# Attention queries in a hybrid encoder: when their tiles are taken

## The chip, the cores and the metric

The kernel runs on one core of a Trainium2 chip. The metric is the device time of one execution in microseconds; the median of several runs is given with its range. A profile of one execution shows when each instruction ran on each engine: TensorE (PE, with its weight loads PEld), VectorE (DVE), ScalarE (ACT), GpSimd (POOL) and SyncE (SP), whose queue issues the DMAs.

## The reference, cut to what matters

One step of a two-layer encoder for a prompt of 2048 positions and a sample of 8 x 16 later positions, with the same weights. The first layer computes two mixers from one projection; the change lies in the queries of the first, and the work around it belongs to the second:

```python
z = rms_norm(h, norm_g) @ w_in
a_q, a_k, a_v, a_g, b_qkv, b_g, b_beta, b_alpha = split_cols(z, AB_WIDTHS)
q = rms_norm(a_q.reshape(Bn, T, A_HEADS, A_HEAD_DIM), q_norm)
k = rms_norm(a_k.reshape(Bn, T, A_KV_HEADS, A_HEAD_DIM), k_norm)
o_a = swa_prompt(q, k, v, sinks)            # sample: swa_sample
...
bq = l2_norm(...); bk = l2_norm(...)
o_b, s_new = gated_delta_rule(bq, bk, bv, beta, g, s0, chunk)
o_b = rms_norm(o_b, o_norm) * silu(b_g)
y = h + concatenate([o_a, o_b]) @ w_out
```

The delta rule solves a unit lower triangular system for each chunk. The second layer takes trailing means over 2 to 16 positions, maps them by groups, and adds them behind a gate.

## The kernel before

The positions are worked on in four groups of 128-row blocks (`GROUPS`). Group 0 holds four prompt blocks (0 to 3) and, as block 4, the sample's 128 rows (`samp`, `npb` = 4 prompt blocks, `nb` = 5); groups 1 to 3 hold four prompt blocks each. Each product is three matmuls, of high and low parts (`XH`, `XL`, and `w` split in two), so that a projection of eight slices of the contraction is 24 matmuls. Weights come two ahead by `weight()`: SyncE loads `wst`, ScalarE makes the high part (L471), VectorE and GpSimd the low part (L475).

A group runs keys, then for each of two pairs of heads the second mixer's keys (`b_keys`), its queries (`b_queries`) and the attention's queries (`a_queries`); for pair 0 `a_queries` stands ahead of `b_queries`, for pair 1 behind it. Then come gate projections (L702 to L704), the output projection and the pooling layer.

`a_queries(jp)` runs over the blocks that `tok_major` yields. For each block there are 24 matmuls, L1305 to L1307, into one of two PSUM banks `pj`. ScalarE copies the bank into the tile `z` (L1400; L1397 for the sample's block) and squares it (L1319). VectorE sums the squares (L1320, L1324 or L1322), GpSimd takes the power -1/2 (L501, tile `rsa`) and scales `z` twice (L1328, L1329). Later `qcols` transposes `z` on TensorE by four matmuls into one of two banks `tp` (L1412), and ScalarE (L1414) and VectorE (L1416) write the high and low part into `qs`. The sample's block goes through L1407 and L1408 into `A`.

Beside it the second mixer runs as jobs. `b_chain` inverts the triangular blocks: VectorE makes 31 steps of two instructions (L1019, L1020) on the tile `Xb`, copies it transposed into `XbT` (L1024), SyncE writes both to DRAM (L1026, L1027) and reads them back in another layout (L1035, L1037), and small matmuls (L1046 to L1081) and copies finish the inverse. Then `b_recur` walks the chunks (L1172 to L1220), and in group 0 also the sample's, one head after the other: L1172, L1241, L1249, L1190, L1255 and L1261 on TensorE, and on VectorE L1182, L1192, L1196, L1198, L1259 and eight L1264, with L1272, then L501 (tile `ro`) and L1277 on GpSimd to end a head. When `a_queries(1)` of group 0 runs, the sample's recurrence of pair 0 and the inverse of pair 1 are under way.

What sets the order: the code emits instructions by hand. `tick` moves a virtual clock on with each projection matmul, and jobs and deferred functions (`defer(DEF, qcols)`) run when they are due. Large SBUF tiles come from `slot`, which has 11 big and 6 small ones in two free lists, first in, first out; `drop` puts one back at the end. Where none is free, `slot` calls `progress`, which runs the next deferred function or job ahead of its due time until one is. A tile that was used before is waited for: its new writer waits for the last readers, DMAs among them. Afterwards each engine's instructions are put in an order of their own by the scheduler of the framework.

Of the kernel before, what the change touches and what calls it, by code (L numbers as in the profile page):

```python
# [8 lines left out]
F32R = mybir.dt.float32r  # L9
# [6 lines left out]
P = 128  # L16
# [221 lines left out]
def hybrid_kernel(  # L238
# [50 lines left out]
    def slot(shape, dt=F32):  # L289
        size = 1  # L290
        for s in shape[1:]:
            size *= s
        while True:
            if size <= SMALL and free_small:
                tag = free_small.pop(0)
                break
            if free_big:
                tag = free_big.pop(0)
                break
            if not progress():  # L300
                raise RuntimeError("no slot: " + ", ".join(v[2] for v in held.values()))
        v = sl.tile(list(shape), dt, tag=tag, name=nm(tag), bufs=1)
        held[id(v)] = (tag, v, str(shape))
        return v
# [5 lines left out]
    def drop(*vs):  # L310
        for v in vs:
            tag = held.pop(id(v))[0]
            (free_big if tag[0] == "B" else free_small).append(tag)
# [366 lines left out]
    def group(gix, norm_job):  # L680
        p0, npb, samp = GROUPS[gix]
# [700 lines left out]

        def a_queries(jp):

            qs = [slot([P, 2, 4, P], F32R) for _ in range(2)]
            zs = [slot([P, 2, 4, 2, 64]) for _ in range(2)]
            A = qh = None
            if samp:

                A = slot([P, 2, n])  # L1390
                qh = A[:, :, srow].rearrange("p c (j q) -> p c j q", q=64)
                zs.append(A[:, 0, 0:256].rearrange("p (j g d) -> p j g d", j=2, d=64))
            st["qh", jp] = (qs, qh, A)
            for b, pp in tok_major():
                z = zs[b // 2][:, b % 2] if b < npb else zs[2]
                if b >= npb:
                    S.copy(z.rearrange("p j g d -> p g j d"), pp.rearrange("p (g j d) -> p g j d", g=2, d=64))  # L1397
                    head_norm(z.rearrange("p j g d -> p (j g) d"), 4)
                else:
                    S.copy(z[:, :, 0, :], pp.rearrange("p (i d) -> p i d", d=64))  # L1400
                    head_norm(z[:, :, 0, :], 4, z[:, :, 1, :], qms[:, 4 * jp:4 * jp + 4])

                def qcols(z=z, b=b):
                    pt = psum("tp")
                    if b >= npb:
                        for j in range(2):
                            T_.transpose(pt[:, P * j:P * j + P], z[:, j].rearrange("p g d -> p (g d)"), ident)  # L1407
                        S.mul(qh.rearrange("p c j q -> p j c q"),  # L1408
                              pt[:, 0:256].rearrange("p (j c q) -> p j c q", j=2, q=64), gq8)
                        return  # L1410
                    for i in range(4):
                        T_.transpose(pt[:, P * i:P * i + P], z[:, i].rearrange("p e d -> p (e d)"), ident)  # L1412
                    q = qs[b // 2][:, b % 2].rearrange("p i t -> p (i t)")
                    S.mul(q, pt, gq8)  # L1414
                    low = q[64:128]
                    V.scalar_tensor_tensor(low, pt[64:128], gq8[64:128], f32(low), op0=ALU.mult,  # L1416
                                           op1=ALU.subtract)

                defer(DEF, qcols)

            def end():
                drop(*zs[0:2])
                st["A", jp] = start(a_attend(jp), 0.6)

            defer(DEF + 0.1, end)
# [450 lines left out]
```

## Time and profile before

| what | value |
|---|---|
| median of 3 runs (range) | 1901.49 us (1900.74 to 1903.12) |
| the profiled execution, its own time | 1898.98 us |
| its span | 1897.2 us |
| mean granted clock of TensorE | 0.992 |

The profile's page gives for each engine the busy time, its share of the span and the count of instructions. The slices cut the span in 40 equal parts, each digit the busy share in tenths. The waits group the idle times of an engine by the instruction behind them and by the one that ended them (total us, times, longest). A timeline row is the start, the duration, the engine, the line, the operation with its tiles (out<-in), and in brackets the idle time ahead of it with what ended it. A window row is its length, then the busy time of TensorE, its weight loads, VectorE, ScalarE and GpSimd, each with a count, then TensorE's clock, the DMA share and GB/s.

### The profile page before, as it was taken

Reading aid. Unit: us, or ns where it says so; the run is one execution under the profiler, and the core shown is the slowest. Engines: PE = TensorE matmul, PEld = TensorE weight load, DVE = VectorE, ACT = ScalarE, POOL = GpSimd, SP = SyncE. Lnnn points to the kernel's source line nnn. Section 1 sums busy time; section 2 is a strip of 40 time slices with the busy share of each in tenths; the row PEclk is TensorE's granted clock in tenths of the full one; section 3 lists DMA queues with packets and bytes.
Section 4 is the critical chain, followed back from the end, with each engine's and each line's share of the span. In section 5 each row is a group of like instructions: output and inputs, shape, how many; then the busy total and the mean of one; then the engine's idle time right before and its main releaser. Section 6 shows DMA issues by size and latency. Waiting matters only on the chain.

```text
span 1897.2 us, 30999 instructions
## 1 busy us (share of the span) xinstructions
PE 1824.5 (96%) x11434; PEld 1598.7 (84%) x11434; DVE 1196.4 (63%) x3184; ACT 733.8 (39%) x1883; POOL 498.8 (26%) x628
## 2 busy tenths in 40 slices
PE   6999989999999999999999999999999999999999
PEld 6888888889998888888888988888888988788887
DVE  6797967545664697764445597774345597764342
ACT  4465436323332474262222374261222474261210
POOL 5632451323332522310112413220012413220100
PEclk9998999999999999999999999999999999999999
DMA  7433362756668533435457533435467533435554
GB/s 277 144 133 125 120 226 76 250 195 208 229 234 293 214 119 105 167 118 189 171 204 282 208 115 108 166 130 188 161 217 278 204 117 118 148 134 189 182 189 186
DMA packets 94579, 337.52 MB, mean 178 GB/s; under 512 B 35884, under 2 KB 44332, under 8 KB 64988
## 3 DMA queue, kind: packets, MB, share of 16 engines
q1 hardware_dynamic: 94428, 335.54, 50.8%
q8 instruction: 90, 1.47, 0.3%
q14 instruction: 61, 0.50, 0.1%
HBM read 256.93 MB, written 78.58 MB: 177 GB/s over the span
## 4 chain that ended last, share of the span: by engine, by line
PE 74%; DVE 16%; POOL 3%; issue 3%; ACT 2%; DMA 2%; SPq 0%; DVEq 0%; POOLq 0%; ACTq 0%
PE pj L702 12%; PE pj L704 12%; PE pj L703 12%; PE pj L737 3%; PE pj L735 3%; PE pj L736 3%; PE rc L737 2%; PE rc L735 2%; PE rc L736 2%; DVE tm L1019 2%; DVE A L1020 2%; PE pj L1305 2%; PE pj L1306 2%; PE pj L1307 2%; PE tp L557 1%
## 5 line engine op out<-in xcount | busy, mean ns | idle before, releaser
L702 PE MATMUL pj<-XH,w 128*128 128x512 f32 (+3 forms) x1512 | 546.9, 362 | 5.5 <-ACT cb L876 3.4
L704 PE MATMUL pj<-XH,w 128*128 128x512 f32 (+3 forms) x1512 | 536.2, 355 | 0.0
L703 PE MATMUL pj<-XL,w 128*128 128x512 f32 (+3 forms) x1512 | 535.1, 354 | 0.0
L702 PEld LDWEIGHTS pj<-XH,w 128*128 128x128 f32 x1512 | 288.2, 191 | 33.7 <-ACT cb L876 3.7
L704 PEld LDWEIGHTS pj<-XH,w 128*128 128x128 f32 x1512 | 287.5, 190 | 29.3 <-issue 0.2
L703 PEld LDWEIGHTS pj<-XL,w 128*128 128x128 f32 x1512 | 288.0, 190 | 26.5 <-issue 0.2
L475 POOL TENSOR_TENSOR w<-wst,w 128x640 fp32r<-128x640 f32 (+2 forms) x60 | 105.2, 1754 | 179.0 <-ACT w L471 154.5
L1305 PE MATMUL pj<-w,XH 128*128 128x256 f32 (+1 forms) x368 | 106.8, 291 | 0.3 <-DVE VL L1351 0.3
L1307 PE MATMUL pj<-w,XL 128*128 128x256 f32 (+1 forms) x368 | 104.4, 284 | 0.0
L1306 PE MATMUL pj<-w,XH 128*128 128x256 f32 (+1 forms) x368 | 104.3, 283 | 0.0
L742 DVE TENSOR_TENSOR A<-pj,A 128x512 f32<-128x512 f32 x37 | 25.5, 689 | 101.4 <-PE pj L737 101.4
L737 PE MATMUL pj<-w,B 128*128 128x512 f32 x224 | 87.5, 391 | 0.0
L737 PE MATMUL rc<-w,B 128*128 128x512 f32 x212 | 82.6, 390 | 0.0
L471 ACT CAST w<-wst 128x1024 fp32r<-128x1024 f32 (+1 forms) x60 | 61.2, 1021 | 53.5 <-PE sc L737 42.0
L1723 DVE TENSOR_TENSOR B<-cb 128x526 f32<-128x526 f32 x32 | 24.1, 752 | 75.8 <-ACT cb L1775 75.7
L475 DVE TENSOR_TENSOR w<-wst,w 128x384 fp32r<-128x384 f32 (+2 forms) x60 | 48.1, 804 | 37.3 <-ACT w L471 37.1
L715 DVE SCALAR_TENSOR_TENSOR A<-A,pj 128x512 f32<-128x512 f32 (+1 forms) x33 | 21.1, 639 | 80.1 <-ACT A L714 79.8
L1305 PEld LDWEIGHTS pj<-w,XH 128*128 128x128 f32 x368 | 70.0, 190 | 1.7 <-DVE VL L1351 0.5
L1306 PEld LDWEIGHTS pj<-w,XH 128*128 128x128 f32 x368 | 70.1, 190 | 1.1 <-issue 0.5
L1307 PEld LDWEIGHTS pj<-w,XL 128*128 128x128 f32 x368 | 70.0, 190 | 0.0
L1019 DVE TENSOR_TENSOR tm<-A,A 40x31 f32<-40x31 f32 (+31 forms) x155 | 62.9, 406 | 6.8 <-DMA A<-Ld 4.4
L896 DVE SCALAR_TENSOR_TENSOR B<-cb,taps,B 128x512 f32<-128x512 f32 x78 | 57.8, 741 | 11.9 <-ACT B L885 11.2
(505 smaller groups left out, 4299.0 us busy)
## 6 DMA issues: line engine op xcount, KB each, us to landing
w<-wk SPq DMA_DIRECT2D x168, 1024.0 KB, 4.9
wk<-w SPq DMA_DIRECT2D x56, 1024.0 KB, 6.4
wst<-in_wts SPq DMA_DIRECT2D x56, 512.0 KB, 4.3
A<-in_x SPq DMA_DIRECT2D x22, 512.0 KB, 4.5
w<-wk SPq DMA_DIRECT2D x6, 1056.0 KB, 5.3
B<-in_x SPq DMA_DIRECT2D x12, 512.0 KB, 4.2
w<-wk SPq DMA_DIRECT2D x12, 512.0 KB, 3.3
out_y<-B SPq DMA_DIRECT2D x9, 512.0 KB, 2.6
```

The costliest lines, as they stand in the source:

```text
L471: S.copy(hi, st)
L475: eng.tensor_tensor(lo[:, a:b], st[:, a:b], f32(hi[:, a:b]), op=ALU.subtract)
L702: mm(pp[:, 0:w], wh[:, k, :], xh[:, k, t0:t1], start=(k == 0), stop=False)
L703: mm(pp[:, 0:w], wh[:, k, :], xl[:, k, t0:t1], start=False, stop=False)
L704: mm(pp[:, 0:w], wl[:, k, :], xh[:, k, t0:t1], start=False, stop=(k == KT - 1))
L735: mm(pp, oh[:, tk], wt[0][:, k, :], start=(kk == k == 0), stop=False)
L736: mm(pp, oh[:, tk], wt[1][:, k, :], start=False, stop=False)
L737: mm(pp, ol[:, tk], wt[0][:, k, :], start=False, stop=(kk == k == 1))
L1019: V.tensor_tensor(t3, bc(Lb[:, j + 1:32, j], w), bcm(Xb[:, j, 0:w], r), op=ALU.mult)
L1305: mm(pp[:, 0:N], xh[:, k, tk], wh[:, k % 4, :], start=(k == 0), stop=False)
L1306: mm(pp[:, 0:N], xh[:, k, tk], wl[:, k % 4, :], start=False, stop=False)
L1307: mm(pp[:, 0:N], xl[:, k, tk], wh[:, k % 4, :], start=False, stop=(k == KT - 1))
```

## The change

The tiles of the queries are no longer taken all at the start of `a_queries`. A pair `qs`, `zs` is taken when an even prompt block comes out of its matmuls, `A` when the sample's block does; and a `zs` is dropped by `qcols` of the odd block that uses it last, no longer by `end` after all of them. The lines behind move: L1397 becomes L1398, L1400 L1401, L1407 L1408, L1412 L1413, L1414 L1415, L1416 L1417.

```diff
--- before.py
+++ after.py
@@ -1382,17 +1382,18 @@
 
         def a_queries(jp):
 
-            qs = [slot([P, 2, 4, P], F32R) for _ in range(2)]
-            zs = [slot([P, 2, 4, 2, 64]) for _ in range(2)]
+            qs, zs = [], []
             A = qh = None
-            if samp:
-
-                A = slot([P, 2, n])
-                qh = A[:, :, srow].rearrange("p c (j q) -> p c j q", q=64)
-                zs.append(A[:, 0, 0:256].rearrange("p (j g d) -> p j g d", j=2, d=64))
-            st["qh", jp] = (qs, qh, A)
             for b, pp in tok_major():
-                z = zs[b // 2][:, b % 2] if b < npb else zs[2]
+                if b == npb:
+
+                    A = slot([P, 2, n])
+                    qh = A[:, :, srow].rearrange("p c (j q) -> p c j q", q=64)
+                    zq = A[:, 0, 0:256].rearrange("p (j g d) -> p j g d", j=2, d=64)
+                if b < npb and b % 2 == 0:
+                    qs.append(slot([P, 2, 4, P], F32R))
+                    zs.append(slot([P, 2, 4, 2, 64]))
+                z = zs[b // 2][:, b % 2] if b < npb else zq
                 if b >= npb:
                     S.copy(z.rearrange("p j g d -> p g j d"), pp.rearrange("p (g j d) -> p g j d", g=2, d=64))
                     head_norm(z.rearrange("p j g d -> p (j g) d"), 4)
@@ -1400,7 +1401,7 @@
                     S.copy(z[:, :, 0, :], pp.rearrange("p (i d) -> p i d", d=64))
                     head_norm(z[:, :, 0, :], 4, z[:, :, 1, :], qms[:, 4 * jp:4 * jp + 4])
 
-                def qcols(z=z, b=b):
+                def qcols(z=z, b=b, qh=qh):
                     pt = psum("tp")
                     if b >= npb:
                         for j in range(2):
@@ -1415,11 +1416,14 @@
                     low = q[64:128]
                     V.scalar_tensor_tensor(low, pt[64:128], gq8[64:128], f32(low), op0=ALU.mult,
                                            op1=ALU.subtract)
+                    if b % 2:
+                        drop(zs[b // 2])
 
                 defer(DEF, qcols)
 
+            st["qh", jp] = (qs, qh, A)
+
             def end():
-                drop(*zs[0:2])
                 st["A", jp] = start(a_attend(jp), 0.6)
 
             defer(DEF + 0.1, end)
```

In group 0, `a_queries(1)` asked for its five tiles with too few free, and `progress` then ran steps of pair 0's sample recurrence of its second head ahead of their time. In the changed code it asks later and for fewer at a time, and none is forced there. The tiles are other ones too, and so the waits and the orders change. Three engines' orders around the query blocks of `a_queries(1)` in group 0 follow; the numbers in a name count tiles, rows with "x3" stand for so many alike, and brackets name the engines or DMA queues that an instruction waits for.

TensorE, from the first query transposes on. Before (the sample's block, `pj_3304`, stands 49 rows ahead of these, its first row being `L1305 MATMUL pj_3304<-w_2870,XH 128x256 [waits Activation_49]`, and its 24 matmuls and 17 of the gate projection `pj_3413` lie between):

```order
L1172 MATMUL rc_3470<-first,B_322_1842 128x128
L1207 MATMUL rc_3470<-S_331,B_322_1842 128x128
L1208 MATMUL rc_3470<-S_331,B_407_2273 128x128
L1172 MATMUL rc_3480<-first,B_322_1842 128x128
L1412 MATMUL tp_3275<-first,B_587_3072 128x128 [waits Activation_49,Pool_49]
L1412 MATMUL tp_3275<-first,B_587_3072 128x128 x3
L1412 MATMUL tp_3317<-first,B_587_3072 128x128 [waits Activation_49,Pool_49]
L1412 MATMUL tp_3317<-first,B_587_3072 128x128 x3
L1207 MATMUL rc_3480<-S_333,B_322_1842 128x128
L1208 MATMUL rc_3480<-S_333,A_455_2489 128x128
L702 MATMUL pj_3413<-XH,w_3084 128x320
L703 MATMUL pj_3413<-XL,w_3084 128x320
```

In the changed order, where `pj_3303` is the sample's block, `tp_3274` and `tp_3316` are blocks 0 and 1, and `sc_3148` belongs to the sample's recurrence of the second head:

```order
L1172 MATMUL rc_3480<-first,B_322_1842 128x128
L1207 MATMUL rc_3480<-S_333,B_322_1842 128x128
L1261 MATMUL sc_3148<-t_3146,kdt_3049 128x512 [waits DVE_49]
L1261 MATMUL sc_3156<-t_3154,kdt_3049 128x512 [waits DVE_49]
L1413 MATMUL tp_3274<-first,B_585_3094 128x128 [waits Activation_49,Pool_49]
L1413 MATMUL tp_3274<-first,B_585_3094 128x128 x3
L1208 MATMUL rc_3480<-S_333,A_455_2489 128x128
L1413 MATMUL tp_3316<-first,B_585_3094 128x128 [waits Activation_49,Pool_49]
L1413 MATMUL tp_3316<-first,B_585_3094 128x128 x3
L1305 MATMUL pj_3303<-w_2870,XH 128x256 [waits PE_49,Activation_49]
L1306 MATMUL pj_3303<-w_2870,XH 128x256
L1307 MATMUL pj_3303<-w_2870,XL 128x256
```

The sample's block, and with it the gate projection, moved from ahead of the transposes of blocks 0 and 1 to behind them, and the second head's L1261 stands directly ahead of them.

ScalarE at the same place. Before, the copies of blocks 2 and 3 (`B_588`) stand ahead of all query transposes' L1414:

```order
L1243 COPY A_563_2971<-sc_3017 128x8x2x16 [waits DMAHW5_49,DMAHW1_49]
L1176 ACTIVATE kdt_3028<-sc_3017,eg_342 128x128
L1185 ACTIVATE qs_3035<-tp_3030,eg_342 128x128 [waits DVE_49]
L1400 COPY B_588_3073<-pj_3196 128x4x64 [waits DMAHW7_49,PE_49]
L1400 COPY B_588_3073<-pj_3262 128x4x64 [waits PE_49]
L1319 ACTIVATE jka_3185<-B_587_3072 128x256 [waits DVE_49,Activation_49]
L471 CAST w_3408<-wst_3082 128x1024 [waits DMAHW6_49,DMAHW3_49,PE_49]
L1397 COPY B_589_3074<-pj_3304 128x2x2x64 [waits PE_49]
```

In the changed order the copies of blocks 2 and 3 (`A_617`):

```order
L1415 ACTIVATE A_584_3093<-tp_3274,gq_310 128x512 [waits PE_49]
L1185 ACTIVATE qs_3476<-rc_3470,eg_342 128x128 [waits DVE_49]
L1176 ACTIVATE kdt_3478<-rc_3470,eg_342 128x128
L1185 ACTIVATE qs_3486<-rc_3480,eg_342 128x128 [waits DVE_49,Activation_49]
L1415 ACTIVATE A_584_3093<-tp_3316,gq_310 128x512 [waits PE_49]
L1176 ACTIVATE kdt_3488<-rc_3480,eg_342 128x128
L1401 COPY A_617_3250<-pj_3193 128x4x64 [waits DMAHW4_49,DMAHW6_49,DMAHW3_49,DVE_49]
L1401 COPY A_617_3250<-pj_3261 128x4x64
```

The copies moved behind L1415 of blocks 0 and 1, and the first of them waits for three DMA queues and VectorE: its tile is the one that `XbT` had.

GpSimd and VectorE. On GpSimd before, with `ro_3069` the second head's end and `rsa_3137`, `rsa_3189` blocks 0 and 1:

```order
L501 TENSOR_TENSOR ro_3069<-so_364_2081,first 128x5 [waits DVE_49]
L1277 TENSOR_TENSOR B_173_1068<-B_173_1068,ro_3069 128x640 [waits Pool_49]
L501 TENSOR_TENSOR rsa_3137<-ssa_3132,first 128x4 [waits DVE_49]
L1328 TENSOR_TENSOR B_587_3072<-B_587_3072,rsa_3137 128x4x64 [waits Activation_49,Pool_49]
L1329 TENSOR_TENSOR B_587_3072<-B_587_3072,rsa_3137 128x4x64 [waits Activation_49,Pool_49]
L475 TENSOR_TENSOR w_3408<-wst_3082,w_3408 128x640 [waits DMAHW6_49,DMAHW3_49,Activation_49]
L1750 COPY cb_5113<-hpool 128x15 [waits DVE_49]
L501 TENSOR_TENSOR rsa_3189<-ssa_3184,first 128x4 [waits DVE_49]
L1328 TENSOR_TENSOR B_587_3072<-B_587_3072,rsa_3189 128x4x64 [waits Pool_49]
L1329 TENSOR_TENSOR B_587_3072<-B_587_3072,rsa_3189 128x4x64 [waits Pool_49]
```

On GpSimd in the changed order, with `rsa_3101`, `rsa_3178` blocks 0 and 1 and `ro_3187` the second head's end:

```order
L501 TENSOR_TENSOR rsa_3101<-ssa_3096,first 128x4 [waits DVE_49]
L1328 TENSOR_TENSOR B_585_3094<-B_585_3094,rsa_3101 128x4x64 [waits Activation_49,Pool_49]
L1329 TENSOR_TENSOR B_585_3094<-B_585_3094,rsa_3101 128x4x64 [waits Activation_49,Pool_49]
L1754 COPY cb_5113<-hpool 128x15 [waits DVE_49]
L501 TENSOR_TENSOR rsa_3178<-ssa_3173,first 128x4 [waits DVE_49]
L501 TENSOR_TENSOR ro_3187<-so_364_2081,first 128x5 [waits DVE_49]
L1328 TENSOR_TENSOR B_585_3094<-B_585_3094,rsa_3178 128x4x64 [waits Pool_49]
L1277 TENSOR_TENSOR B_173_1068<-B_173_1068,ro_3187 128x640 [waits Pool_49]
L1329 TENSOR_TENSOR B_585_3094<-B_585_3094,rsa_3178 128x4x64 [waits Activation_49,Pool_49]
```

The second head's L501 and L1277 moved from ahead of block 0 into block 1's scaling. On VectorE in the changed order, with `tp_3316` block 1 and `A_612` the tile `XbT`:

```order
L1019 TENSOR_TENSOR tm_3120<-A_493_2639,A_494_2641 40x135 [waits DVE_49]
L1020 TENSOR_TENSOR A_494_2641<-A_494_2641,tm_3120 40x5x27 [waits DVE_49]
L1417 SCALAR_TENSOR_TENSOR A_584_3093<-tp_3316,gq_310,A_584_3093 64x512 [waits Activation_49]
L1019 TENSOR_TENSOR tm_3130<-A_493_2639,A_494_2641 40x112 [waits DVE_49]
L1020 TENSOR_TENSOR A_494_2641<-A_494_2641,tm_3130 40x4x28 [waits DVE_49]
L1019 TENSOR_TENSOR tm_3163<-A_493_2639,A_494_2641 40x87 [waits DVE_49]
L1020 TENSOR_TENSOR A_494_2641<-A_494_2641,tm_3163 40x3x29 [waits DVE_49]
L1019 TENSOR_TENSOR tm_3190<-A_493_2639,A_494_2641 40x60 [waits DVE_49]
L1020 TENSOR_TENSOR A_494_2641<-A_494_2641,tm_3190 40x2x30 [waits DVE_49]
L1019 TENSOR_TENSOR tm_3200<-A_493_2639,A_494_2641 40x31 [waits DVE_49]
L1020 TENSOR_TENSOR A_494_2641<-A_494_2641,tm_3200 40x31 [waits DVE_49]
L1024 COPY A_612_3221<-A_494_2641 40x32x32 [waits DMAHW3_49,DVE_49]
```

Block 1's L1417 stands ahead of the last four steps of the inverse (outputs of 4, 3, 2 and 1 rows) and of L1024; before, L1416 of block 0 stands ahead of the last step and that of block 1 between its two instructions.

## The prediction

> **What bounds the kernel now.** I read the page first: the busy shares and the slices.
>
> ```profile
> span 1897.2 us, 30999 instructions
> PE 1824.5 (96%) x11434; PEld 1598.7 (84%) x11434; DVE 1196.4 (63%) x3184; ACT 733.8 (39%) x1883; POOL 498.8 (26%) x628
> ...
> PE   6999989999999999999999999999999999999999
> ```
>
> TensorE is busy for 1824.5 of 1897.2 us, so only 72.7 us of its idle time can be won, and the only digits under 9 are those of the first slice and of the sixth, 237 to 285 us. The change issues no matmul less and moves no data less; it can only move that idle time. So I went to the waits of TensorE (total, times, longest):
>
> ```profile
> PE tp L1412 <- POOL B L1329: 6.0, 3, 3.4
> PE tp L1412 <- DVE A L1416: 5.6, 3, 1.9
> ```
>
> and from there to the windows of 10 us in group 0:
>
> ```profile
> 230.00:240.00 10.00, 9.07 (x72) 8.57 (x73) 9.23 (x32) 2.33 (x7) 5.12 (x3) 1.00 0.66 232
> 240.00:250.00 10.00, 9.98 (x72) 8.88 (x70) 9.62 (x30) 4.09 (x7) 7.36 (x4) 1.00 0.71 256
> 250.00:260.00 10.00, 4.57 (x27) 3.69 (x24) 9.11 (x18) 3.90 (x11) 9.53 (x12) 0.83 0.51 173
> ```
>
> The transposes of the queries, L1412, are among TensorE's largest waits. The 6.0 us behind GpSimd are all in group 0, in `a_queries(1)`; the 5.6 us behind VectorE are one wait of 1.9 us in each of groups 1 to 3. In the windows (length, then TensorE, weight loads, VectorE, ScalarE, GpSimd, clock, DMA) VectorE is nearly full for 20 us, 9.23 and 9.62 of 10, and GpSimd is full just after it, 9.53, where TensorE falls to 4.57. This stage is set by VectorE and GpSimd, and there the change bites.
>
> ```profile
> 246.79 0.31 PE L702 MATMUL pj<-XH,w 128*128 128x320 f32 x1
> ...
> 252.17 0.66 PE L1412 MATMUL tp<-first,B 128*128 128x128 f32 x4 [1.12 <-POOL B L1329]
> 256.20 0.68 PE L1412 MATMUL tp<-first,B 128*128 128x128 f32 x4 [3.37 <-POOL B L1329]
> 260.62 1.12 PE L1412 MATMUL tp<-first,B 128*128 128x128 f32 x4 [1.56 <-POOL B L1329]
> 263.40 0.67 PE L1412 MATMUL tp<-first,B 128*128 128x128 f32 x4
> ```
>
> Before, all five token blocks are through at 246.79, when the gate projection starts. Only then do blocks 0 to 3 stop TensorE, for 1.12, 3.37, 1.56 and no us. At 264.1 (263.40 + 0.67) five blocks, 30 matmuls of the gate projection and four blocks' transposes are done. I compare the changed order with this state.
>
> **The change, part by part.** (1) *Late tiles, no early demand.* Before, `a_queries(1)` of group 0 asks for five tiles at once, finds too few and forces the sample recurrence of the second head ahead of its due time. Afterwards it asks for two at blocks 0 and 2 and one at block 4, and forces nothing. So in GpSimd's order the end of that head (L501 on `ro`, L1277) moves from ahead of block 0 into the middle of block 1. It neither saves nor adds an instruction.
>
> (2) *Which tile comes.* The tile that is free for `z` of blocks 2 and 3 is the one that held the transposed inverse, written by L1024 and read by the DMA of L1026. Block 2's copy into `z`, L1401 (L1400 before), has to wait for that DMA. Block 4's matmuls go into the projection bank that this copy empties, as there are two such banks. So block 4, and the gate projection that is queued behind it, stand behind a chain through all engines. The rows of the orders, shown with the change, say so: TensorE does block 1's transposes, then block 4; ScalarE does block 1's L1415, then block 2's copy; VectorE does block 1's L1417, then the last four steps of the inverse and L1024.
>
> The chain's start. On VectorE the updates of the second head's sample state, L1264, end at 240.75 + 2.15 = 242.9:
>
> ```profile
> 240.75 2.15 DVE L1264 SCALAR_TENSOR_TENSOR A<-A,eg,sc 128x128 f32<-128x128 f32 x8
> 243.16 0.74 DVE L896 SCALAR_TENSOR_TENSOR B<-cb,taps,B 128x512 f32<-128x512 f32 x1
> 244.10 0.40 DVE L1320 TENSOR_REDUCE ssa<-jka 128x4 f32<-128x256 f32 x1
> 244.67 0.15 DVE L1324 SCALAR_TENSOR_TENSOR ssa<-ssa,others 128x4 f32<-128x4 f32 x1
> 248.60 0.81 DVE L901 SCALAR_TENSOR_TENSOR B<-t,B 128x640 f32<-128x640 f32 x1
> ```
>
> In both orders the inverse (L1019, L1020) has come to the same step there, the one of 9 by 23. But the changed order has three L896, the L901 and L1320 with L1324 of blocks 0 and 1 ahead of that point, which before come after it: 3 x 0.74 + 0.81 + 2 x 0.55 = 4.1 us. VectorE was full, so this is time: block 1's sums are ready at 242.9 + 4.1 = **247.0**.
>
> From there one thing waits for the next:
>
> ```profile
> 243.06 2.15 POOL L501 TENSOR_TENSOR ro<-so,first 128x5 f32<-128x5 f32 x1 [2.57 <-DVE so L1272]
> 245.28 2.47 POOL L1277 TENSOR_TENSOR B<-B,ro 128x640 f32<-128x640 f32 x1
> 247.71 2.56 POOL L501 TENSOR_TENSOR rsa<-ssa,first 128x4 f32<-128x4 f32 x1
> ...
> 257.59 1.01 POOL L501 TENSOR_TENSOR rsa<-ssa,first 128x4 f32<-128x4 f32 x1
> ...
> 262.30 0.61 POOL L1329 TENSOR_TENSOR B<-B,rsa 128x256 f32<-128x256 f32 x1
> ...
> L1277 POOL TENSOR_TENSOR B<-B,ro x4: 1257/1504/2466, 235.7 to 346.7; 128x640 f32<-128x640 f32 x4
> ```
>
> GpSimd must do block 1's L501, the head's L501, block 1's L1328 (the twin of L1329, of the same shape), the head's L1277 and block 1's L1329. Beside a full VectorE that is 2.56 + 2.15 + 0.61 + 2.47 + 0.61 = 8.4 us; by the shortest rows 1.01 + 1.01 + 0.61 + 1.26 + 0.61 = 4.5 us. I take 6.5, between them: the first two run beside a full VectorE, the rest beside one that waits.
>
> The Trainium skill, in the page "SBUF — State Buffer", section "SBUF: two separate sides", says that VectorE and GpSimd share a port pair under an exclusive lock, so that the engine that comes second stands until the other's instruction ends. By that rule GpSimd would run at its short times as soon as VectorE stands, and the chain would be nearer 4.5, which makes the sum below 2 us smaller; the rows speak for both, since the one L501 took 2.56 and the other 1.01 us.
>
> ```profile
> 252.86 0.69 ACT L1414 ACTIVATE A<-tp,gq 128x512 fp32r<-128x512 f32 x1 [1.11 <-PE tp L1412]
> 255.63 0.76 DVE L1416 SCALAR_TENSOR_TENSOR A<-tp,gq,A 64x512 fp32r<-64x512 f32 x1
> 253.93 0.23 DVE L1020 TENSOR_TENSOR A<-A,tm 40x87 f32<-40x87 f32 x1
> 258.97 1.21 DVE L1024 COPY A<-A 40x1024 f32<-40x1024 f32 x1
> 260.21 0.29 SPq L1026 DMA_DIRECT2D Xd<-A  x1
> 263.69 0.32 SPq L1035 DMA_DIRECT2D B<-Xd  x1
> 239.53 0.37 ACT L1400 COPY B<-pj 128x256 f32<-128x256 f32 x1 [1.72 <-PE pj L1307]
> ```
>
> Then the transposes 0.67, L1415 as L1414 took 0.69, L1417 as L1416 took 0.76: 2.1 us. The last four steps of the inverse are eight instructions like the L1020 of 0.23, 1.9 us, and L1024 is 1.21. The DMA of L1026 is issued at 260.21, and SyncE's first read of what it wrote at 263.69: 3.5 us. The copy is 0.37 (the row is block 2's of before, which starts when its matmuls end, with no DMA in its way). Together 6.5 + 2.1 + 1.9 + 1.2 + 3.5 + 0.4 = 15.6 us (13.6 to 17.5 by GpSimd's ends). Block 4 starts at 247.0 + 15.6 = **262.6** (260.6 to 264.5). In all this time TensorE has only the two blocks' transposes to do.
>
> To the state of before there lack 24 matmuls of block 4, 30 of the gate projection and two blocks' transposes.
>
> ```profile
> 242.83 0.28 PE L1305 MATMUL pj<-w,XH 128*128 128x256 f32 x1
> 242.95 0.28 PE L1306 MATMUL pj<-w,XH 128*128 128x256 f32 x1
> ...
> 246.94 0.31 PE L703 MATMUL pj<-XL,w 128*128 128x320 f32 x1
> ...
> 261.80 0.47 PE L702 MATMUL pj<-XH,w 128*128 128x320 f32 x1
> 262.06 0.47 PE L703 MATMUL pj<-XL,w 128*128 128x320 f32 x1
> ```
>
> By the starts that is 24 x 0.12 + 30 x 0.15 + 2 x 0.67 = 8.7 us: 271.3 against 264.1, **+7.2**. After a stall the same 320 columns came every 0.26 in place of 0.15 us. Some 3 us of this half pace follow the new, longer stall too, +1.5 us, the size of what the 11 or so slow matmuls already cost before (11 x 0.11 = 1.2 us), so of this I add only 0.5: **+7.7**.
>
> (3) *What else moves.* The rest of the inverse (L1046 to L1083) follows block 4 closely, where before about 75 projection matmuls lie between; each of its steps waits for a copy or a DMA. The work is not more, the waits may be 0 to 3 us; against it stands that the inverse is done sooner, for recurrences that wait later:
>
> ```profile
> PE sc L1261 <- DVE t L1259: 2.2, 3, 0.8
> PE tp L1536 <- DVE kd L1535: 1.0, 1, 1.0
> ```
>
> These waits of the second pair's sample recurrence come to 3.2 us. I set the two against each other: 0, with -3 and +3 kept for the range.
>
> (4) *`a_queries(0)`, and the groups 1 to 3.* No job is forced in either order, and around the 1.9 us waits at L1412 the order of the transposes and their neighbours is the same before and after. `z` comes free two blocks sooner, and nothing waits for it there. I count 0; bounds from the two nearest waits, -1.9 to +1.9 a group, kept to 2 us in all.
>
> The sum is +7.7 us on the profiled run's 1898.98 us (its span of 1897.2 and 1.8 around it), 1906.7. That run lies 2.5 us below the median of the runs shown, 1901.49; timed runs are to be compared with the median, which gives 1909.2. Of GpSimd's two ends the shorter is a little likelier, since VectorE stands for most of the chain, so I round down: **1908.0**.
>
> **The rivals.** *Faster.* The forced recurrence bunches GpSimd's work beside VectorE's, and instructions of both are stretched there:
>
> ```profile
> 226.00 1.76 DVE L1019 TENSOR_TENSOR tm<-A,A 40x255 f32<-40x255 f32 x1
> ...
> 228.54 0.41 DVE L1019 TENSOR_TENSOR tm<-A,A 40x256 f32<-40x256 f32 x1
> ```
>
> The same step of the inverse took 1.76 and 0.41 us. If three such stretches go, VectorE's part is ready 4 us sooner, at 243, and GpSimd runs at its short times. It decides by block 4's start: 264.1 - 8.7 - 0.5 = 254.9 is the point below which the stage gains. The chain of 13.6 from 243 gives 256.6, +1.7; with the 3.2 us of later waits gone, and 2 us of (4), it ends at 1.7 - 3.2 - 2 = -3.5, and with the groups' further bounds at -5: 1896 to 1898. For it: the 6.0 us behind GpSimd do go. Against it: it needs every short time at once.
>
> *Even.* The one wait takes the place of the three: GpSimd at its short times (chain 13.6), and VectorE ready 2 us sooner by half of the stretches. Then block 4 starts at 245.0 + 13.6 = 258.6, +3.7, and the later waits take up to 3 of it back: +0.7 to +3.7, 1902 to 1905.
>
> *Still slower.* The steps of the inverse, L1046 to L1083, find no cover and stop TensorE again, 3 us, and GpSimd runs at its long times, 1.9 us: 7.7 + 4.9 = 12.6 us, 1914.
>
> **How the numbers follow.** The forecast has 0.53, still slower 0.12, even 0.21, faster 0.14. A measurement of this kernel tells about 0.2% from no change, 3.8 us: 1897.7 to 1905.3. Slower holds the forecast and its stronger form, 0.65; within the bound is even, 0.21; faster 0.14. Eight in ten needs the even case and the stronger case whole, and the faster one down to its middle: 1897 to 1915.
>
> **What would show it.** In the changed profile: one wait of TensorE of 10 us or more just ahead of a block of L1305 near 262, put down to ScalarE or to the DMA behind it; L1401 there with an idle time of some us; L1417 of block 1 ahead of L1024 on VectorE; L1277 between block 1's L1328 and L1329. TensorE's sum of that window falls from 4.57 to near nothing. It is wrong if L1024 ends before 254, if L1401 waits for no DMA, or if groups 1 to 3 change by more than 2 us.

## The result, and the profile after

| | before | changed |
|---|---|---|
| median of the compared runs (range) | 1900.37 us (1898.54 to 1903.12), 6 runs | 1907.63 us (1904.79 to 1910.43), 6 runs |
| the profiled execution, its own time | 1898.98 us | 1908.54 us |
| its span | 1897.2 us | 1906.8 us |
| mean granted clock of TensorE | 0.992 | 0.987 |

The ratio is 1.0032, with a 95% interval of 1.0022 to 1.0043: slower, by 6 us by the ratio and by 7 by the medians. The forecast was 1908.0 us, in a range of 1897 to 1915. The sum came out; whether its terms did is another question.

The page after, busy shares and slices:

```profile
span 1906.8 us, 31025 instructions
PE 1824.9 (96%) x11434; PEld 1601.1 (84%) x11434; DVE 1199.1 (63%) x3184; ACT 733.6 (38%) x1883; POOL 492.6 (26%) x628
...
PE   6999969999999999999999999999999999999998
```

The work is the same: TensorE's busy time grew by 0.4 us, the span by 9.6. The dip of the sixth slice is deeper, 6 where it was 8. The waits of TensorE (total, times, longest; from 206 us, behind the queries of pair 0, to 428 us) name what stands there:

```profile
PE tp L1413 <- POOL B L1329: 8.8, 1, 8.8
PE pj L1305 <- ACT A L1401: 7.7, 1, 7.7
PE tp L1540 <- DVE kd L1539: 2.1, 1, 2.1
```

Where three waits of 6.0 us in all stood behind GpSimd there are two of 8.8 and 7.7 us in a row, 16.5 us with 1.12 us of transposes between them. The timelines of TensorE, GpSimd, ScalarE, VectorE and SyncE show the chain (start, duration, engine, line, in brackets the idle time ahead):

```profile
254.00 1.12 PE L1413 MATMUL tp<-first,B 128*128 128x128 f32 x4 [8.75 <-POOL B L1329]
262.85 0.58 PE L1305 MATMUL pj<-w,XH 128*128 128x256 f32 x1 [7.74 <-ACT A L1401]
...
249.01 1.13 POOL L501 TENSOR_TENSOR rsa<-ssa,first 128x4 f32<-128x4 f32 x1 [5.54 <-DVE so L1272]
250.11 1.34 POOL L501 TENSOR_TENSOR ro<-so,first 128x5 f32<-128x5 f32 x1
251.42 0.61 POOL L1328 TENSOR_TENSOR B<-B,rsa 128x256 f32<-128x256 f32 x1
251.99 1.33 POOL L1277 TENSOR_TENSOR B<-B,ro 128x640 f32<-128x640 f32 x1
253.28 0.66 POOL L1329 TENSOR_TENSOR B<-B,rsa 128x256 f32<-128x256 f32 x1
...
255.16 0.69 ACT L1415 ACTIVATE A<-tp,gq 128x512 fp32r<-128x512 f32 x1 [3.38 <-PE tp L1413]
262.43 0.65 ACT L1401 COPY A<-pj 128x256 f32<-128x256 f32 x2 [6.33 <-DMA Xd<-A]
...
234.16 0.35 DVE L1182 SCALAR_TENSOR_TENSOR R<-tp,nb,B 128x128 f32<-128x128 f32 x1 [4.63 <-PE tp L1249]
248.78 0.14 DVE L1324 SCALAR_TENSOR_TENSOR ssa<-ssa,others 128x4 f32<-128x4 f32 x1
252.24 1.23 DVE L1019 TENSOR_TENSOR tm<-A,A 40x135 f32<-40x135 f32 x1
255.88 0.76 DVE L1417 SCALAR_TENSOR_TENSOR A<-tp,gq,A 64x512 fp32r<-64x512 f32 x1 [1.78 <-ACT A L1415]
256.67 0.27 DVE L1019 TENSOR_TENSOR tm<-A,A 40x112 f32<-40x112 f32 x1
258.75 1.05 DVE L1024 COPY A<-A 40x1024 f32<-40x1024 f32 x1
...
259.82 0.29 SPq L1026 DMA_DIRECT2D Xd<-A  x1
```

Read from the end. Block 4's matmuls start at 262.85, as soon as ScalarE has copied block 2 out of the bank. That copy stood 6.33 us for the DMA that reads L1024's tile (`Xd<-A`), issued at 259.82, behind L1024, behind the last four steps of the inverse, behind L1417 of block 1, behind its transposes, which stood 8.75 us for GpSimd; and GpSimd's L1277 lies between block 1's L1328 and L1329. Every link is the one forecast.

The windows of 10 us (length, TensorE, weight loads, VectorE, ScalarE, GpSimd, clock, DMA share, GB/s):

```profile
220.00:230.00 10.00, 7.73 (x54) 7.36 (x52) 9.53 (x26) 3.02 (x9) 4.28 (x4) 0.87 0.48 155
230.00:240.00 10.00, 10.00 (x69) 10.00 (x69) 5.84 (x16) 3.01 (x8) 3.21 (x3) 0.79 0.21 86
250.00:260.00 10.00, 1.12 (x4) 0.72 (x4) 7.54 (x19) 1.87 (x5) 4.30 (x6) 0.50 0.21 68
260.00:270.00 10.00, 7.15 (x46) 6.86 (x47) 1.72 (x5) 2.97 (x7) 5.50 (x7) 0.50 0.26 51
```

From 250 to 260 TensorE falls to 1.12 of 10 us (4.57 before). Two things were not forecast. From 220 to 240 the granted clock is 0.87 and 0.79, where it was 1.00, and VectorE, which the forecast took to be full, has 5.84 of 10: it stands 4.63 us for a product of TensorE at 234.16. And the clock stays at 0.50 to 270, where the forecast had some 3 us of half pace.

To see where the 9.6 us arise I cut the span at two places that stand alike in every kernel here: cut 1 where the last L1112 waits for L901, behind the queries of pair 0, and cut 2 where group 0 ends and an L557 waits. Before:

```profile
210.04 1.38 PE L1112 MATMUL sc<-A,B 128*128 128x128 f32 x10 [1.47 <-DVE A L901]
417.51 0.55 PE L557 MATMUL tp<-first,B 128*128 128x128 f32 x3 [0.36 <-DVE B L1697]
```

Changed:

```profile
206.61 1.35 PE L1112 MATMUL sc<-A,B 128*128 128x128 f32 x10 [0.63 <-DVE A L901]
426.59 0.55 PE L557 MATMUL tp<-first,B 128*128 128x128 f32 x3 [0.37 <-DVE B L1701]
```

Up to cut 1 the changed kernel is 3.4 us **ahead**. Between the cuts it needs 220.0 us in place of 207.5, 12.5 more. Behind cut 2 both need 1480 (0.5 us apart). So -3.4 + 12.5 + 0.5 = +9.6: two effects of opposite sign.

### The profile page after: what moved, and what is told of

The parts are those of the page before. It is cut to its first block, busy times and chain, and to the rows that moved or that the text cites. A ratio compares the mean times of both kernels' runs of the same rounds, so it can differ in the third digit from the quotient of the medians.

```text
span 1906.8 us, 31025 instructions
## 1 busy us (share of the span) xinstructions
PE 1824.9 (96%) x11434; PEld 1601.1 (84%) x11434; DVE 1199.1 (63%) x3184; ACT 733.6 (38%) x1883; POOL 492.6 (26%) x628
## 4 chain that ended last, share of the span: by engine, by line
PE 74%; DVE 15%; ACT 4%; issue 3%; POOL 2%; DMA 1%; SPq 0%; DVEq 0%; ACTq 0%; POOLq 0%
PE pj L704 12%; PE pj L702 12%; PE pj L703 12%; PE pj L737 3%; PE pj L735 3%; PE pj L736 3%; PE rc L737 2%; PE rc L736 2%; PE rc L735 2%; DVE tm L1019 2%; PE pj L1306 2%; PE pj L1305 2%; PE pj L1307 2%; DVE A L1020 1%; DVE B L896 1%
## 5 line engine op out<-in xcount | busy, mean ns | idle before, releaser
L702 PE MATMUL pj<-XH,w 128*128 128x512 f32 (+3 forms) x1512 | 543.3, 359 | 2.4 <-DVE VL L1351 1.0
L702 PEld LDWEIGHTS pj<-XH,w 128*128 128x128 f32 x1512 | 286.8, 190 | 30.5 <-DVE B L715 1.4
L1305 PE MATMUL pj<-w,XH 128*128 128x256 f32 (+1 forms) x368 | 108.4, 295 | 8.7 <-ACT A L1401 8.3
L1306 PE MATMUL pj<-w,XH 128*128 128x256 f32 (+1 forms) x368 | 107.0, 291 | 0.3 <-DVE w L475 0.3
L1307 PE MATMUL pj<-w,XL 128*128 128x256 f32 (+1 forms) x368 | 106.5, 289 | 0.0
L742 DVE TENSOR_TENSOR B<-pj,B 128x512 f32<-128x512 f32 x48 | 33.1, 691 | 104.5 <-PE pj L737 104.4
L896 DVE SCALAR_TENSOR_TENSOR B<-cb,taps,B 128x512 f32<-128x512 f32 x90 | 69.8, 776 | 20.3 <-ACT B L885 19.5
L1305 PEld LDWEIGHTS pj<-w,XH 128*128 128x128 f32 x368 | 72.1, 196 | 10.1 <-ACT A L1401 8.9
L737 PE MATMUL pj<-w,B 128*128 128x512 f32 x200 | 78.2, 391 | 0.0
L737 PE MATMUL rc<-w,B 128*128 128x512 f32 x188 | 73.2, 390 | 0.0
L1306 PEld LDWEIGHTS pj<-w,XH 128*128 128x128 f32 x368 | 72.2, 196 | 1.1 <-DVE w L475 0.5
L1307 PEld LDWEIGHTS pj<-w,XL 128*128 128x128 f32 x368 | 72.2, 196 | 0.0
L1019 DVE TENSOR_TENSOR tm<-A,A 40x31 f32<-40x31 f32 (+31 forms) x155 | 62.5, 403 | 2.1
```

What stands on the lines that cost most here:

```text
L702: mm(pp[:, 0:w], wh[:, k, :], xh[:, k, t0:t1], start=(k == 0), stop=False)
L737: mm(pp, ol[:, tk], wt[0][:, k, :], start=False, stop=(kk == k == 1))
L896: V.scalar_tensor_tensor(dst[:, 0:Tp], cb[:, j:j + Tp], taps[:, m, j:j + 1], dst[:, 0:Tp], op0=ALU.mult, op1=ALU.add)
L1019: V.tensor_tensor(t3, bc(Lb[:, j + 1:32, j], w), bcm(Xb[:, j, 0:w], r), op=ALU.mult)
L1305: mm(pp[:, 0:N], xh[:, k, tk], wh[:, k % 4, :], start=(k == 0), stop=False)
L1306: mm(pp[:, 0:N], xh[:, k, tk], wl[:, k % 4, :], start=False, stop=False)
```

## The experiments

Each time stands beside runs of the kernel before on the same chip, whose median was 1900.92 to 1901.62 us. The experiments are told in the order in which they explain the result.

### One call at a time

`a_queries` is called eight times. In three kernels only some calls take their tiles late and give `z` back early; the others do as before:

```diff
         def a_queries(jp):
+            late = samp and jp == 1
...
+            if not late:
+                qs.extend(slot([P, 2, 4, P], F32R) for _ in range(2))
+                zs.extend(slot([P, 2, 4, 2, 64]) for _ in range(2))
+                if samp:
+                    A, qh, zq = take_a()
...
-                    if b % 2:
+                    if late and b % 2:
                         drop(zs[b // 2])
...
             def end():
+                if not late:
+                    drop(*zs)
```

With this condition only `a_queries(1)` of group 0 is late, the call on which the prediction rests:

> The change in a_queries(1) of group 0 alone; all other calls take their tiles as before. Theory: all of the loss is made there, so 1905 to 1909, with the two waits of the changed kernel (8.8 and 7.7 us, within 1 us). Rival (the loss comes from the other calls, whose tiles also change): 1899 to 1902.

1909.48 us (1908.08 to 1912.25), ratio 1.0045 (1.0032 to 1.0058), 0.5 us over the range expected and far from the rival's. The two waits are there, by the waits of this kernel (206 to 428 us):

```profile
PE pj L1305 <- ACT A L1413: 5.8, 1, 5.8
PE tp L1425 <- POOL B L1329: 5.2, 1, 5.2
```

(L1425 and L1413 are L1413 and L1401 of the changed kernel.) Their sizes are not those of the changed kernel, 5.2 and 5.8 in place of 8.8 and 7.7, so this part of the expectation missed. Alone this call costs 0.45%, 8.5 us, and 7.2 us between the cuts (211.68 to 426.34, 214.7 us).

All calls but that one, `late = not (samp and jp == 1)`:

> The change everywhere but in a_queries(1) of group 0, which takes its tiles at the start as before. Theory: no wait at L1305 in that stage; within 0.2% of before, 1897 to 1904. Rival (the other calls cost): 1905 or more.

1890.32 us (1888.32 to 1896.88), ratio 0.9946 (0.9933 to 0.9959). It was expected at no change, and it is **faster by half a per cent**. The rest of the change, which the prediction set at nothing, holds a gain of 10 us. Two more kernels divide it. First `late = samp and jp == 0`, the queries of pair 0 in group 0 alone:

> a_queries(0) of group 0 alone takes its tiles by two and gives z back early; all other calls as before. Theory (the unforeseen gain of the kernel with all but a_queries(1) of group 0 sits in this one call, groups 1 to 3 are worth nothing, as step (4) said of them): ratio 0.994 to 0.996, 1889 to 1894 us, the first idle row of L1112 behind L901 near 207 as there. Rival (groups 1 to 3 hold part of it): 1895 us or more.

1889.30 us (1888.55 to 1890.10), ratio 0.9941 (0.9928 to 0.9954): the whole gain is in this one call. Then groups 1 to 3 alone, `late = not samp`:

> groups 1 to 3 alone take their tiles late; group 0 as before. Step (4): within 2 us of before, ratio 0.999 to 1.001. Rival (the earlier return of z changes the tiles of the groups too): a difference of 3 us or more, to either side.

1900.68 us (1899.24 to 1902.04), ratio 0.9999 (0.9991 to 1.0008): no change to be seen, as step (4) said of the groups.

What did the one call bring? The cuts of its trace are at 206.72 and 406.10: 3.3 us up to cut 1, and 199.4 in place of 207.5 us behind it, 8.1. A good half of the first part can be read in the stretch of 140 to 160 us. Before, in TensorE's timeline and in a window:

```profile
145.05 0.64 PE L702 MATMUL pj<-XH,w 128*128 128x320 f32 x1 [3.42 <-ACT cb L876]
```

```profile
140.00:160.00 20.00, 15.15 (x96) 13.94 (x95) 13.82 (x39) 10.33 (x30) 7.53 (x6) 0.74 0.61 192
```

With the one call late, the same two:

```profile
154.65 0.42 PE L702 MATMUL pj<-XH,w 128*128 128x320 f32 x1 [1.14 <-ACT cb L876]
```

```profile
140.00:160.00 20.00, 15.94 (x120) 14.65 (x120) 14.65 (x35) 12.07 (x31) 9.62 (x8) 0.91 0.80 268
```

TensorE's wait at L702 shrinks by 2.3 us, and the clock of the stretch rises from 0.74 to 0.91: 120 instructions of TensorE run there in place of 96. It is not only a gain: TensorE waits 2.92 us at L1516 in this stretch, where it waited 1.03 at the same line (L1498) before. The other 1.5 us are there already near 120, where another L1112 that waits for L901 starts at 119.34 us, before at 120.83.

The second part is GpSimd's timeline where `a_queries(1)`, as it was, works on its blocks, in this kernel:

```profile
238.17 1.17 POOL L501 TENSOR_TENSOR ro<-so,first 128x5 f32<-128x5 f32 x1 [3.99 <-DVE so L1272]
239.42 1.49 POOL L1277 TENSOR_TENSOR B<-B,ro 128x640 f32<-128x640 f32 x1
240.88 1.16 POOL L501 TENSOR_TENSOR rsa<-ssa,first 128x4 f32<-128x4 f32 x1
```

Before, the same three began at 243.06, 245.28 and 247.71 and took 2.15, 2.47 and 2.56 us. Now the last begins 6.8 us sooner (3.3 of them are those ahead of cut 1), and the three take 3.8 us in place of 7.2. A window there:

```profile
250.00:260.00 10.00, 7.79 (x55) 7.25 (x56) 8.68 (x24) 5.10 (x11) 7.57 (x11) 1.00 0.46 158
```

TensorE has 7.79 us at a clock of 1.00, where it had 4.57 at 0.83.

### Which part of that call

The kernel before, where `a_queries(0)` of group 0 takes all its tiles at the start as ever and only gives each `z` back two blocks sooner:

```diff
+                    if b % 2 and samp and not jp:
+                        drop(zs[b // 2])
...
             def end():
-                drop(*zs[0:2])
+                if not (samp and not jp):
+                    drop(*zs)
```

> The kernel before, with one line of the change alone: in a_queries(0) of group 0 a z tile is given back with the odd block that uses it last, and not at the end. All tiles are taken at the start as before. Theory (this earlier return, which hands small tiles to the jobs behind it, made the run with the change everywhere but in group 0's pair 1 faster): 1888 to 1893. Rival (there the later taking of the tiles was the gain): 1898 to 1903.

1892.85 us (1892.21 to 1896.03), ratio 0.9958 (0.9945 to 0.9970). Most of the gain is the early return. Its cuts are at 210.31 and 411.08: it has the gain between the cuts (200.8 us), not the 3 us ahead of them (+0.3), so those belong to the late taking. (The profiled execution is the slowest of the five, 1896.03 us; the time that it has more lies behind cut 2.) A single `drop`, put earlier, hands a tile to a job of the second mixer sooner and shifts which tile each later job gets; nothing that is computed differs.

### The sample's tile

The changed kernel, but the sample's output tile `A` taken at the start as before:

```diff
             A = qh = None
+            if samp:
+                A = slot([P, 2, n])
...
             for b, pp in tok_major():
-                if b == npb:
-                    A = slot([P, 2, n])
```

> The pairs qs and z by two blocks as in the change, the sample's tile A taken at the start as before. Theory: the earlier demand for A shifts the tiles, block 2's z is a big tile that no DMA of the inverse reads, so no wait for the inverse stands ahead of block 4; 1897 to 1903. Rival (taking q and z by two is what costs, whatever tile comes): 1905 or more.

1899.52 us (1896.33 to 1901.62), ratio 0.9991 (0.9982 to 0.9999), as expected. Both long waits go; in their place stand 5.7 us at L1138 behind L901 and 3.5 us at L1261 behind L1259. So the late `A` makes the difference between this and the changed kernel, 8 us. Like every edit here it shifts later tiles too, so the 8 us are not the one wait's alone.

### The tile that waits for the DMA

The changed kernel, with the inverse's two tiles given back later, in all calls:

```diff
             Q.dma_start(Xd[1].rearrange("b c i j -> (b c) i j"), Xb)
-            drop(Xb, XbT)
...
             yield XTW
+            drop(Xb, XbT)
```

> The changed kernel, but the tiles of the inverse (Xb and its transposed copy) are given back one wait later, after the reads of what was written, so that block 2's z in a_queries(1) of group 0 gets another tile (a big one). Theory (the reused tile): the copy of block 2 waits for its matmuls alone, the wait of 7.7 us at L1305 is gone, block 4 stands ahead of the transposes, and one wait of 3 to 6 us at L1413 for GpSimd's L1329 stays; the time is that of before or a little less, 1896 to 1901. Rival (the second head's recurrence, no longer forced early, is what costs): GpSimd's order is that of the changed kernel, so the waits stay 12 us or more in sum and the time 1905 or more.

1910.80 us (1910.43 to 1911.43), ratio 1.0050 (1.0038 to 1.0062): missed. The wait at L1305 is gone, but TensorE's waits (206 to 428 us) read:

```profile
PE tp L1413 <- POOL B L1329: 8.0, 2, 5.0
PE sc L1519 <- DVE A L1586: 2.9, 1, 2.9
PE sc L1112 <- DVE A L901: 1.5, 1, 1.5
```

The edit also held tiles back for pair 0. The last row shows it: cut 1, with its wait of 1.5 as before, is at 211.59, so the gain ahead of it is lost too. And between the cuts it needs 215.9 us, no less than the kernel with pair 1 alone (214.7), in which the wait at L1305 stands: other waits came in its place. It changes several things at once and decides nothing. So I did it once more for the second pair in group 0 alone:

```diff
-            drop(Xb, XbT)
+            if not (samp and pr):
+                drop(Xb, XbT)
...
             yield XTW
+            if samp and pr:
+                drop(Xb, XbT)
```

> The changed kernel, with the inverse's two tiles given back one wait later in pair 1 of group 0 alone, so that nothing else shifts as it did in the run that kept them everywhere (there pair 0 lost 2.5 us at L1054 and 2.9 at L1519 to demands for tiles). Block 2's z is then a big tile that no DMA reads; block 4 stands ahead of block 1's transposes. Theory (the reused tile): the 7.7 us at L1305 are gone, at most 5 us at the transposes stay, and the time is 1895 to 1901. Rival (the second head's late end on GpSimd): sums and scaling of block 1 come no sooner, the waits in that stage stay over 10 us, and the time is 1905 or more.

1900.67 us (1897.78 to 1901.94), ratio 0.9994 (0.9985 to 1.0002). The reused tile's wait at L1305 is gone and with it 7 us, all that the change cost against the kernel before. What is left of the two is the wait behind GpSimd, 6.5 us where at most 5 were expected:

```profile
PE tp L1416 <- POOL B L1332: 6.5, 2, 5.5
```

A wait of 2.4 us at L1522 (the 2.9 at L1519 of the run above), which the changed kernel does not have, comes with this edit also. So it belongs to pair 1's tiles, and not to pair 0 as the expectation had it.

### The head's end on GpSimd

The changed kernel, but the head's end (L1272, `ro`, L1277) comes later in the program, so that it falls behind block 1's L1329:

```diff
+            if samp and not pr:
+                yield 2.5
             for e in range(2):
                 so2 = so2s[e]
```

> The changed kernel, with the end of the sample recurrence of pair 0 (L501 on ro and the scaling of the output) due 2.5 us later in group 0, so that on GpSimd it comes behind block 1's scaling and no longer inside it; TensorE's and ScalarE's orders at that place stay as they are. Theory (a chain of VectorE, GpSimd, inverse and DMA): the chain is shorter by those two instructions, 1.3 + 1.3 us, so the wait at the transposes falls from 8.8 to some 6, the one at L1305 stays at 7.7, and the time is 1904 to 1906. Rival (the head's end is the main cause): the wait falls by 6 us or more, under 1901.

1903.34 us (1901.55 to 1905.46), ratio 1.0009 (1.0000 to 1.0018), 0.7 us under the theory's range and 2.3 above the rival's. GpSimd goes from L501 straight to block 1's scalings, and the wait at the transposes falls from 8.8 to 6.2 us, as expected; the one at the projection is 8.4 for an expected 7.7. But TensorE's rows show more (lines here are 2 higher, L1415 for L1413 and L1307 for L1305):

```profile
226.81 1.97 PE L1241 MATMUL sc<-t,A 128*128 128x32 f32 x16 [1.22 <-DVE t L1237]
...
247.85 1.12 PE L1415 MATMUL tp<-first,B 128*128 128x128 f32 x4 [6.21 <-POOL B L1331]
257.36 0.58 PE L1307 MATMUL pj<-w,XH 128*128 128x256 f32 x1 [8.39 <-ACT A L1403]
```

Cut 1 lies at 206.98 here, so block 4 starts 50.4 us behind it, in the changed kernel 56.2 (262.85 - 206.61). Of this difference of 5.9 us the chain from VectorE's sums to block 4 gives 1.9 (12.0 for 13.9 us) and the sums 4.0: they are ready 38.3 us behind cut 1, in the changed kernel 42.3. And here the wait at L1241 is 1.22 us, and the clock 1.00 from 220 to 240. The edit moved more than the head's end: GpSimd's L1030, which fills a tile of the inverse, stood at 226.05 us in the changed kernel and stands at 250.29 here. That this makes the 4.0 us is read further down.

Both edits together, the inverse's tiles of the second pair and the head's end:

> Both: the inverse's tiles kept longer in pair 1 of group 0, and the head's end behind block 1's scaling. Theory: as the run that keeps the tiles, and up to 2.7 us less, 1893 to 1900. Rival (the head's end): under 1901 here as in the run that moves it alone, and no less than there.

1897.80 us (1893.01 to 1901.08), ratio 0.9977 (0.9968 to 0.9986), as expected, with 6.6 us in three waits behind GpSimd. It is a little faster than the kernel before, and slower than the kernel with the one late call.

### The changed kernel once more

The clock of 0.87 and 0.79 from 220 to 240 might have belonged to one execution:

> The changed kernel once more, for a second profile. If the wait of some 2 us at L1241 near 227 and the half pace that follows it (granted clock under 0.9 from 220 to 240) belong to its order, they are there again, and block 4 starts 56 us behind the L1112 that waits for L901, as in the first profile. If they belonged to that one execution, the wait is near 1 us, the clock 1.00, and block 4 starts some 51 us behind. Time 1905 to 1910 in either case.

1909.59 us (1904.15 to 1911.06), ratio 1.0042 (1.0031 to 1.0054). The second profile, in TensorE's timeline and a window:

```profile
228.13 2.65 PE L1241 MATMUL sc<-t,A 128*128 128x32 f32 x16 [2.13 <-DVE cvs L887]
```

```profile
230.00:240.00 10.00, 10.00 (x62) 10.00 (x63) 6.15 (x17) 3.01 (x8) 3.40 (x3) 0.70 0.31 125
```

The wait of 2.13 us, the lower clock behind it (0.96, then 0.70) and VectorE's gap (6.15 of 10) are there again, and block 4 starts 55.6 us behind cut 1 (262.85 - 207.23). They belong to the order. Between the cuts this execution took 217.3 us, the first 220.0, though block 4 starts at the same time in both: the clock of 260 to 270 was 0.66 here and 0.50 there. So a cut's figure holds to about 3 us.

## Why the prediction was right, and where its sum was not

The mechanism is shown: a tile whose last reader is a DMA put block 4 behind a chain through all engines. Without that tile the wait at L1305 is gone and the time is that of before (1900.67 us), and the call alone costs what the sum gave (7.2 us between the cuts; the sum said 7.7), though with shorter waits. It is not all that this call costs. Against the kernel that lacks only this call's change (1890.32 us) the changed kernel needs 17 us more: other tiles for the inverse take back 7 of them, these and the later head's end 10, and the rest was not taken apart.

The terms, one by one, in the changed kernel:

| step | forecast | measured |
|---|---|---|
| (2) VectorE's sums of block 1 ready | 247.0, 37.0 behind cut 1 | 248.92, 42.3 behind it |
| GpSimd's five instructions | 6.5 (4.5 to 8.4) | 4.9 (249.01 to 253.94) |
| transposes, L1415, L1417 | 2.1 | 2.6 (254.00 to 256.64) |
| last four steps, then L1024 | 1.9 + 1.2 | 2.0 + 1.05 (256.67 to 259.80) |
| DMA, to the start of the copy | 3.5 | 2.6 (259.82 to 262.43) |
| copy | 0.4 | 0.4 |
| block 4 starts | 262.6, 52.6 behind cut 1 | 262.85, 56.2 behind it |
| (4) `a_queries(0)` | 0 | -3.4 ahead of cut 1 |

Block 4's time agrees to 0.3 us because two errors cancel, which is luck: the stage began 3.4 us sooner and took 3.6 us longer.

**The ready time** was mis-sized, +5.3 us. The prediction took VectorE for full up to there ("VectorE was full, so this is time"). It was full before; in the changed order TensorE waited longer at L1241 and ran at half pace behind it, L1241 itself took 3.62 us, and VectorE stood 4.63 us for TensorE. Where that wait is 1.22 us (the kernel with the later head's end) VectorE stands 1.11 us there and the sums come 38.3 us behind cut 1, near the 37.0 forecast. TensorE before:

```profile
232.49 1.97 PE L1241 MATMUL sc<-t,A 128*128 128x32 f32 x16 [0.93 <-DVE t L1237]
```

TensorE, GpSimd and VectorE in the changed kernel:

```profile
227.35 3.62 PE L1241 MATMUL sc<-t,A 128*128 128x32 f32 x16 [2.13 <-DVE cvs L887]
226.05 1.17 POOL L1030 MEMSET B<- 128x1280 f32 x1 [1.84 <-DVE t L1236]
226.17 1.13 DVE L1237 COPY t<-B 128x128 f32<-128x128 f32 x1
```

VectorE with the later head's end:

```profile
226.54 0.21 DVE L1237 COPY t<-B 128x128 f32<-128x128 f32 x1
```

L1241 needs what L1237 copies. In the changed kernel GpSimd's fill L1030 runs beside this copy, and the copy takes 1.13 us, 0.9 more; that is the difference of the two waits, 2.13 and 1.22. VectorE's standing behind it, 4.63 for 1.11 us, is 3.5 of the 4.0 us by which the sums differ. It is so in all thirteen profiles: L1237 takes 1.12 or 1.13 us in the five where L1030 stands beside it (both of the changed kernel, pair 1 alone, and the two that only keep the inverse's tiles), 0.21 in the eight where it stands elsewhere. The fill stands beside the copy in every kernel here in which `a_queries(1)` of group 0 takes all its tiles late and the head's end is not moved: it is an effect of the change that the prediction did not see. An edit that moves L1030 alone was not run.

**GpSimd's chain** was mis-sized by 1.6 us. It ran near its short end, but the reason that the prediction gave, that VectorE stands for most of the chain, does not hold: VectorE was at work from 249 to 254. The prediction drew on a rule of the Trainium skill (page "SBUF — State Buffer", section "SBUF: two separate sides"): where VectorE and GpSimd both need the port pair that they share, the one that comes second stands until the other's instruction ends. The trace agrees, with VectorE as the second: L1277 began at 251.99, and the L1019 that began beside it at 252.24 took 1.23 us where the next, somewhat smaller one, at 256.67, took 0.27. Which of the two engines pays is not to be read from how full VectorE is.

**The half pace behind block 4** was mis-sized. The prediction let 3 us of it follow and added 0.5. Block 4's 24 matmuls with the 20 small L1046 between them took from 262.85 to 269.64 us (6.8), where 2.9 and 0.8 (L1046 in the kernel with the later head's end) would do: some 3.1 us. Seven more matmuls, of the gate projection, came every 0.27 in place of 0.15 us up to 271.51: 0.8. Before, the slow matmuls had cost 1.2, so 2.7 had to be added.

With these the stage's sum is 7.7 + 5.3 - 1.7 (the chain, 13.9 for 15.6) + 2.2 (2.7 for 0.5) = 13.5. Between the cuts 12.5 were measured in this execution; the 9.8 of the second (217.3 for 207.5) show that such a sum is good to some 3 us.

**Step (3)**, the later waits, was right near 0. L1540 rose from 1.0 to 2.1 us and L1261 behind L1259 and L1272 fell from 2.2 to 1.6. The steps of the inverse did not stop TensorE for long, so the rival "still slower" did not come to its price by that way. "Faster" and "even" had GpSimd's short times right, but wanted VectorE ready 4 and 2 us sooner, and it was later.

**Step (4)** failed for `a_queries(0)`, and held for groups 1 to 3. The sentence was: "`z` comes free two blocks sooner, and nothing waits for it there. I count 0". The bound was 2 us in all; alone this call is worth -11 us (ratio 0.9941). The argument looked for someone waiting for that tile, and for a changed order around the transposes; the effect lies in which tiles the jobs behind get, and shows near 145 us and again near 240, while the call's own projection runs near 70.

So the total met the time by luck, because errors cancelled. Nor do the parts add: -0.59% (pair 0 alone), +0.45% (pair 1 alone) and 0 (the groups) make -0.14%, and the whole has +0.32% and +0.42%. The gain of the one call between the cuts (8.1 us) lies where `a_queries(1)` takes all its tiles at the start and the head's end is through GpSimd before the blocks' scalings. With that call late, as in the changed kernel, the head's end lies among the scalings, and of pair 0's gain only the 3.4 us ahead of cut 1 are left. This is read from the traces of the two kernels. The longer wait at L1241 (1.18 us with pair 1 alone, 2.13 with both) is no effect of pair 0's tiles on that copy: L1237 takes 1.12 us with pair 1 alone too, but there TensorE comes later, as it waits 0.94 us at L1306 just ahead.

## What to carry to other kernels

Before taking a tile later or giving it back sooner, ask which tile of the pool comes next, and what its last reader is: where that is a DMA, the new writer and all that is queued behind it wait for the transfer and for what feeds it. In a first in, first out pool every edit changes the tiles of all later jobs, so each call is to be measured alone, and, as the parts do not add, with the others; here one call held a gain of 0.6% and the next a loss of 0.45%. The best version measured, 1889.30 us, beats both kernels: late tiles in `a_queries(0)` of group 0, all else as before.

## What the runs showed of the hardware

A wait of TensorE of 2.13 us cost more than itself: granted clocks of 0.87 and 0.79 in the two windows behind it (0.96 and 0.70 in the second profile), against 1.00 behind one of 1.22 us at the same place. The one wait's length does not settle it: with pair 1 alone, waits of 0.84, 0.94 and 1.18 us within 6 us were followed by 0.75 from 240 to 250. After 16.5 us of near standstill the clock was 0.50 from 260 to 270 in one execution, and 0.66 over the same window in the other.

GpSimd's fill L1030 took 1.17 us, and L1237, L1019 and L887 of VectorE, which ran beside it, 1.13, 1.00 and 0.74 us, where with the later head's end, and the fill elsewhere, they took 0.21, 0.39 and 0.16.

The write of L1026 and the release of its tile took 2.6 us from the issue to the copy; the 3.5 us taken from before were the distance to SyncE's next read, not the time of the write.
